# Chaining the partial sums of the seven Strassen-Winograd products in PSUM, with a ScalarE copy from bank to bank

## Chip, cores and metric

The kernel runs on one core of a Trainium2 chip. The metric is the device time of one execution in microseconds (us), median of three runs.

## The reference

Two transformer layers over 1024 tokens of 1024 features, in float32: forgetting attention, SwiGLU, retention, SwiGLU, each behind an RMS norm and with a residual, and a last norm. The change touches the SwiGLU stages and the projections of the retention:

```python
def swiglu(h, w_in, w_out):
    gu = h @ w_in
    return (jax.nn.silu(gu[..., :D_FF]) * gu[..., D_FF:]) @ w_out      # D_FF = 2816

def retention(h, w_in, w_out):
    proj = h @ w_in                          # q 1024, k 1024, v 2048, g 2048 columns
    q, k, v, g = ...                         # 4 heads; q and k are rotated
    ...                                      # chunkwise recurrence
    return (jax.nn.silu(g) * y) @ w_out
```

## The kernel before

Every operand is the sum of two float32r tiles, `hi` and `lo`. `split` writes them: ScalarE casts `hi` (L98), VectorE subtracts to get `lo` (L99). A product of two operands is three matmuls (hi·hi, hi·lo, lo·hi), lines L638, L639 and L640. Weights come by DMA into `st` tiles (five buffers) and are split into `wh` and `wl` tiles (six buffers each), 512 columns at a time. Activations are split into `b` tiles, which stay for a whole stage.

The large matrix products go by Strassen-Winograd. The weights of a pair of 128-column tiles are four blocks A11, A12, A21, A22 with the sums S1 to S4; the activations are four blocks B11 to B22 with the sums T1 to T4. Seven products of twelve matmuls (128x128 weights on 512 tokens) make the four blocks of the result C11, C12, C21, C22. Three PSUM banks take them: A11·B11 and A12·B21 accumulate in bank a, which is C11; S2·T2, S3·T3 and A22·T4 accumulate in bank b; S1·T1 and S4·B22 in bank c. The order is the table `PRODUCTS`: A11, S2, S1, S3, A12, S4, A22.

Bank b holds no result by itself. P1, the first product, belongs to C12, C21 and C22 too. So ScalarE copies bank a after its first product into an SBUF tile `p1` (L699), and VectorE adds `p1` to what bank b holds after S2 (`u2`, L702), after S3 (`u3`, L706) and after A22 (L713). Bank c is added after S1 (L708) and after S4 (L711).

`pair_T` does so for the 22 pairs of each SwiGLU's first matrix (`ffn`, 44 in all) and for 16 pairs of the retention's projections (`rotated`, `gates`). `pair_N` does the same token-major with 256-column weights for the values (4 pairs, two banks for each of a, b, c; L737 to L739). `pair_acc` and `paired_out` do the second SwiGLU matrix, whose activations are kept in memory as sums (`Stored`) and come back through `st` tiles: two groups of four pairs for each SwiGLU, `first` telling the group that writes the sums `y` (copies by ScalarE, L653) from the one that adds to them (VectorE, L650).

Banks come from one pool of seven in turn (`mm_ps`); three are in use for a pair. The program is written in dependence order; a scheduler of the language sets the order of the instructions on each engine, and each engine runs its own list in order.

Of the kernel before, what the change touches and what calls it, by code (L numbers as in the profile page):

```python
# [17 lines left out]
P = 128  # L18
# [19 lines left out]
def trunk(ctx, tc, nc, d, out):  # L38
# [145 lines left out]
    # =================== forgetting attention ===================  # L184
    with ExitStack() as fs:
# [230 lines left out]
        # the keys of the first two heads, a pass over the features as they come  # L416
# [79 lines left out]
    # where the sums of a phase are kept  # L496
# [41 lines left out]
    class Stored:  # L538
        """The sums of a group of four pairs of feature tiles, kept in memory, split at their first use."""
# [29 lines left out]
    class Blocks:  # L569
        """The four blocks of a pair of column tiles and their sums, split on demand."""  # L570
# [25 lines left out]
        def get(self, n):  # L596
# [13 lines left out]
            if n == "S4":  # L610
# [4 lines left out]
    PRODUCTS = (("A11", "B11", "a"), ("S2", "T2", "b"), ("S1", "T1", "c"), ("S3", "T3", "b"),  # L615
                ("A12", "B21", "a"), ("S4", "B22", "c"), ("A22", "T4", "b"))

    class Products:
        """The seven products of one pair of 128-column tiles, feature-major."""

        def __init__(self, src, X):
            self.w, self.X, self.banks = src if isinstance(src, Blocks) else Blocks(src), X, {}

        def __call__(self, i):
            n, t, bk = PRODUCTS[i]
            if n == "S2" and not self.w.s1:
                self.w.sums()
            hi, lo = self.w.get(n)
            tt = self.X.get(t)
            new = bk not in self.banks  # L630
            if new:
                self.banks[bk] = mm_ps()
            ps = self.banks[bk]
            for j in range(4):
                js = slice(j * P, (j + 1) * P)
                th, tl = tt[j]
                f = new and j == 0
                nc.tensor.matmul(ps, hi[:, js], th, start=f, stop=False, skip_group_check=not new)  # L638
                nc.tensor.matmul(ps, hi[:, js], tl, start=False, stop=False, skip_group_check=not new)  # L639
                nc.tensor.matmul(ps, lo[:, js], th, start=False, stop=(j == 3), skip_group_check=not new)  # L640

    def pair_acc(src, X, y, first):
        """Adds the products of one pair to the sums y over the groups of feature tiles."""
        prod = Products(src, X)
        banks = prod.banks
        if first:
            y.update({n: yu(n) for n in ("11", "12", "21", "22")}, p=qu("p"))

        def add(n, bk):
            nc.vector.tensor_tensor(y[n], banks[bk], y[n], op=ALU.add)  # L650

        def put(n, bk):
            nc.scalar.copy(y[n], banks[bk]) if first else add(n, bk)  # L653

        prod(0)
        put("p", "a")
        prod(1)
        put("12", "b")
        prod(2)
        prod(3)  # L660
        put("22", "b")
        add("22", "c")
        prod(4)
        put("11", "a")
        prod(5)
        add("12", "c")
        prod(6)
        put("21", "b")

    def paired_out(wsrc, stored, scale_rows, xold):  # L670
        """x + (scaled) act @ W over the groups of eight feature tiles whose sums are in memory."""
        ys = [{} for _ in range(4)]
        out = [[None, None] for _ in range(KT)]
        for g, X in enumerate(stored):
            for n in range(4):
                y = ys[n]
                pair_acc(wsrc[g, n], X, y, g == 0)
                if g < len(stored) - 1:
                    continue
                for q in ("12", "21", "22"):  # L680
                    nc.vector.tensor_tensor(y[q], y[q], y["p"], op=ALU.add)
                for i in range(2):
                    for h in range(2):
                        u = y[f"{i + 1}{h + 1}"]
                        if scale_rows:
                            nc.vector.tensor_tensor(u, u, R[:, HALF[h]], op=ALU.mult)
                        xo = sp.tile([P, H], F32, tag="xo", name=nm("xo"), bufs=2)
                        nc.sync.dma_start(xo, xold[2 * n + i][:, HALF[h]])
                        nc.vector.tensor_tensor(u, u, xo, op=ALU.add)
                        out[2 * n + i][h] = u  # L690
        return out

    def pair_T(src, X):
        """Feature-major C11, C12, C21, C22 of one pair of 128-column tiles."""
        prod = Products(src, X)
        banks = prod.banks
        prod(0)
        p1 = yu("p1")
        nc.scalar.copy(p1, banks["a"])  # L699
        prod(1)  # L700
        u2 = yu("u2")
        nc.vector.tensor_tensor(u2, banks["b"], p1, op=ALU.add)  # L702
        prod(2)
        prod(3)
# [4 lines left out]
        prod(4)  # L709
        prod(5)  # L710
        nc.vector.tensor_tensor(u2, banks["c"], u2, op=ALU.add)  # L711
        prod(6)
        nc.vector.tensor_tensor(p1, banks["b"], p1, op=ALU.add)  # L713
        return banks["a"], u2, p1, c22, u3

    def pair_N(srcs, X):
        """Token-major C11, C12, C21, C22 of one pair of 256-column tiles, as two tiles of two token blocks."""
        ws = [Blocks(s) for s in srcs]
        banks = {}

        def prod(n, t, bk):
            parts = [w.get(n) for w in ws]
            new = bk not in banks
            if new:
                banks[bk] = [mm_ps(), mm_ps()]
            for s in range(2):
                ps = banks[bk][s]
                for b in range(2):
                    o = ps[:, b * 256:(b + 1) * 256]
                    tk = slice((2 * s + b) * P, (2 * s + b + 1) * P)  # L730
                    for j in range(4):
                        hi, lo = parts[j // 2]
                        js = slice(j % 2 * 256, (j % 2 + 1) * 256)
                        th, tl = X.get(t)[j]
                        f = new and j == 0 and b == 0
                        sk = not (new and b == 0)
                        nc.tensor.matmul(o, th[:, tk], hi[:, js], start=f, stop=False, skip_group_check=sk)  # L737
                        nc.tensor.matmul(o, th[:, tk], lo[:, js], start=False, stop=False, skip_group_check=sk)  # L738
                        nc.tensor.matmul(o, tl[:, tk], hi[:, js], start=False, stop=(j == 3), skip_group_check=sk)  # L739

        prod(*PRODUCTS[0])
        p1 = [yu("p1"), yu("p1")]
        for s in range(2):
            nc.scalar.copy(p1[s], banks["a"][s])
        for w in ws:
            w.sums()
        prod(*PRODUCTS[1])
        u2, u3, c22 = [[yu(x), yu(x)] for x in ("u2", "u3", "c22")]
        for s in range(2):
            nc.vector.tensor_tensor(u2[s], banks["b"][s], p1[s], op=ALU.add)  # L750
        prod(*PRODUCTS[2])
        prod(*PRODUCTS[3])
        for s in range(2):
            nc.vector.tensor_tensor(u3[s], banks["b"][s], p1[s], op=ALU.add)
            nc.vector.tensor_tensor(c22[s], banks["c"][s], u3[s], op=ALU.add)
        prod(*PRODUCTS[4])
        prod(*PRODUCTS[5])
        for s in range(2):
            nc.vector.tensor_tensor(u2[s], banks["c"][s], u2[s], op=ALU.add)
        prod(*PRODUCTS[6])  # L760
        for s in range(2):
            nc.vector.tensor_tensor(p1[s], banks["b"][s], p1[s], op=ALU.add)
            nc.scalar.copy(u3[s], banks["a"][s])
        return u3, u2, p1, c22
# [489 lines left out]
```

## Time and profile before

| | |
|---|---|
| runs | 2626.6, 2627.21, 2629.64 us (median 2627.21) |
| profiled execution, span of the trace | 2626.0 us |
| median of the runs less that span | 1.2 us |
| TensorE busy | 2600.0 us (99%) |
| VectorE busy | 1960.2 us (75%) |
| ScalarE busy | 1155.9 us (44%) |
| 490 to 910, 1960 to 2375 us | first matrix of the two SwiGLUs |
| 910 to 1075, 2375 to 2545 us | second matrix, paired part |
| 1150 to 1610 us | projections of the retention |

The span is the time from the first to the last instruction of one profiled execution; the profile gives no other time of it. Busy time of an engine is the union of its instructions; a matmul's end is modelled, so TensorE counts as busy as long as matmuls follow each other closely.

### The profile page before, as it was taken

To read this page: it belongs to the slowest core of one execution; us is meant where nothing else is said; L and a number is where in the kernel's file an instruction comes from. 1 tells how busy PE (TensorE), PEld (TensorE's weight loads), DVE (VectorE), ACT (ScalarE), POOL (GpSimd) and SP (SyncE) were. 2 spreads that over 40 slices of the span, in tenths; PEclk is the share of its full clock that TensorE was granted. 3 is DMA by queue.
4 is the path that set the end of the run, shared out by engine and by line. 5 is a ranking of instruction groups with operands and counts; after the bars stand their busy time and mean duration, and the time that the engine had idled before them with its cause. 6 is when DMAs were issued, how large, how long until landed. Compare 5 with 4: busy or idle time off the path is not lost.

```text
span 2626.0 us, 35148 instructions
## 1 busy us (share of the span) xinstructions
PE 2600.0 (99%) x12808; PEld 2179.9 (83%) x12808; DVE 1960.2 (75%) x3367; ACT 1155.9 (44%) x2168; POOL 167.6 (6%) x147
## 2 busy tenths in 40 slices
PE   9999999999999999999999999999999999999998
PEld 8878887888888878889898989898888888887888
DVE  6798888877767778987667676885567776768795
ACT  6566666533233444453333425662353233335533
POOL 0143322000000000001000010000000000000000
PEclk9999999999999999999999999999999999999999
DMA  3111143332332345533332325655522332325441
GB/s 129 44 57 65 49 145 119 122 106 95 109 104 97 109 152 180 167 107 117 104 113 96 113 101 160 189 196 192 190 85 85 104 111 86 109 84 183 156 158 65
DMA packets 137694, 312.11 MB, mean 119 GB/s; under 512 B 15665, under 2 KB 28721, under 8 KB 137521
## 3 DMA queue, kind: packets, MB, share of 16 engines
q1 hardware_dynamic: 136800, 309.33, 35.1%
q8 instruction: 100, 1.64, 0.3%
q14 instruction: 74, 0.60, 0.1%
q10 hardware_dynamic: 720, 0.55, 0.1%
HBM read 217.54 MB, written 92.27 MB: 118 GB/s over the span
## 4 chain that ended last, share of the span: by engine, by line
PE 89%; DMA 4%; DVE 3%; issue 2%; ACT 1%; POOL 0%; SPq 0%; DVEq 0%; POOLq 0%; ACTq 0%
PE mm L638 17%; PE mm L640 17%; PE mm L639 17%; PE mm L106 7%; PE mm L107 7%; PE mm L108 7%; PE mm L738 2%; PE mm L739 2%; PE mm L737 2%; DMA st<-vd 1%; DMA st<-ac_T 1%; PE mm L256 1%; PE mm L258 1%; PE mm L257 1%; DVE b L99 1%
## 5 line engine op out<-in xcount | busy, mean ns | idle before, releaser
L639 PE MATMUL mm<-b,wh 128*128 128x512 f32 x2128 | 836.8, 394 | 0.0
L638 PE MATMUL mm<-b,wh 128*128 128x512 f32 x2128 | 832.9, 395 | 3.2 <-ACT 22_4397_22190 L653 1.8
L640 PE MATMUL mm<-b,wl 128*128 128x512 f32 x2128 | 819.5, 394 | 0.1
L98 ACT CAST wh<-st 128x512 fp32r<-128x512 f32 (+1 forms) x449 | 275.2, 616 | 578.4 <-PE mm L639 409.4
L638 PEld LDWEIGHTS mm<-b,wh 128*128 128x128 f32 x2128 | 400.3, 188 | 97.8 <-ACT 22_4397_22190 L653 2.2
L640 PEld LDWEIGHTS mm<-b,wl 128*128 128x128 f32 x2128 | 399.8, 188 | 94.1 <-DVE wl L99 0.9
L639 PEld LDWEIGHTS mm<-b,wh 128*128 128x128 f32 x2128 | 400.0, 188 | 91.9 <-DVE b L99 0.2
L99 DVE TENSOR_TENSOR wl<-st,wh 128x512 fp32r<-128x512 f32 (+1 forms) x449 | 311.5, 697 | 55.8 <-ACT wh L98 51.8
L98 ACT CAST wh<-s 128x512 fp32r<-128x512 f32 x252 | 156.0, 621 | 413.3 <-PE mm L639 356.8
L106 PE MATMUL mm<-b,wh 128*128 128x512 f32 x736 | 289.7, 397 | 8.4 <-ACT b L126 5.7
L107 PE MATMUL mm<-b,wh 128*128 128x512 f32 x736 | 290.0, 395 | 1.4 <-DVE b L99 1.4
L108 PE MATMUL mm<-b,wl 128*128 128x512 f32 x736 | 289.9, 395 | 0.0
L99 DVE TENSOR_TENSOR wl<-s,wh 128x512 fp32r<-128x512 f32 x252 | 182.6, 727 | 41.4 <-ACT wh L98 39.7
L106 PEld LDWEIGHTS mm<-b,wh 128*128 128x128 f32 x736 | 138.9, 189 | 40.5 <-ACT b L126 6.5
L107 PEld LDWEIGHTS mm<-b,wh 128*128 128x128 f32 x736 | 138.8, 189 | 32.0 <-DVE b L99 1.8
L108 PEld LDWEIGHTS mm<-b,wl 128*128 128x128 f32 x736 | 138.7, 188 | 31.5
L98 ACT CAST b<-st 128x512 fp32r<-128x512 f32 (+1 forms) x216 | 125.1, 612 | 81.7 <-DMA st<-ac_T 30.0
L99 DVE TENSOR_TENSOR b<-st,b 128x512 fp32r<-128x512 f32 (+1 forms) x216 | 140.0, 674 | 27.9 <-ACT b L98 22.5
L711 DVE TENSOR_TENSOR u<-mm,u 128x512 f32<-128x512 f32 x60 | 41.4, 689 | 116.1 <-PE mm L640 115.9
L738 PE MATMUL mm<-wl,b 128*128 128x256 f32 x448 | 126.0, 281 | 0.0
L739 PE MATMUL mm<-wh,b 128*128 128x256 f32 x448 | 125.9, 281 | 0.0
L737 PE MATMUL mm<-wh,b 128*128 128x256 f32 x448 | 125.8, 281 | 0.0
(514 smaller groups left out, 3965.2 us busy)
## 6 DMA issues: line engine op xcount, KB each, us to landing
st<-ffn_in SPq DMA_DIRECT2D x88, 512.0 KB, 3.5
st<-ffn_out_pairs SPq DMA_DIRECT2D x32, 512.0 KB, 5.4
st<-ac_T SPq DMA_DIRECT2D x32, 512.0 KB, 4.6
ac_T<-t SPq DMA_DIRECT2D x48, 256.0 KB, 2.4
st<-ac_B SPq DMA_DIRECT2D x24, 512.0 KB, 4.6
st<-fox_qk SPq DMA_DIRECT2D x32, 256.0 KB, 2.7
xo<-xd SPq DMA_DIRECT2D x32, 256.0 KB, 3.1
ac_B<-p SPq DMA_DIRECT2D x32, 256.0 KB, 3.1
```

Of the source, the lines that this page charges most:

```text
L98: nc.scalar.copy(hi, src)
L99: return nc.vector.tensor_tensor(lo, src, hi.bitcast(F32), op=ALU.subtract)
L106: nc.tensor.matmul(ps, wh, xh, start=(first and k == 0), stop=False)
L107: nc.tensor.matmul(ps, wh, xl, start=False, stop=False)
L108: nc.tensor.matmul(ps, wl, xh, start=False, stop=(last and k == n - 1))
L638: nc.tensor.matmul(ps, hi[:, js], th, start=f, stop=False, skip_group_check=not new)
L639: nc.tensor.matmul(ps, hi[:, js], tl, start=False, stop=False, skip_group_check=not new)
L640: nc.tensor.matmul(ps, lo[:, js], th, start=False, stop=(j == 3), skip_group_check=not new)
L711: nc.vector.tensor_tensor(u2, banks["c"], u2, op=ALU.add)
L737: nc.tensor.matmul(o, th[:, tk], hi[:, js], start=f, stop=False, skip_group_check=sk)
L738: nc.tensor.matmul(o, th[:, tk], lo[:, js], start=False, stop=False, skip_group_check=sk)
L739: nc.tensor.matmul(o, tl[:, tk], hi[:, js], start=False, stop=(j == 3), skip_group_check=sk)
```

## The change

The seven products keep their operands. Their order and the place of the sums change. After A11 ScalarE copies bank a into bank b, from PSUM to PSUM (L642 of the kernel after), and S2, S3 and A22 accumulate onto that copy, so that bank b holds P1+S2, then P1+S2+S3, then all four. `u2` and `u3` are then ScalarE copies of bank b in between (L669, L666), and VectorE adds only bank c to them. C11 and C21 are read from the banks by whoever uses them, and no `p1` tile is left. The order of a pair becomes A11, copy, S1, S2, copy `u2`, A12, S3, copy `u3`, then A11 of the next pair (`open`), and only then A22 and S4 (`close`). `pair_N`'s order is A11, S1, S2, A12, S3, A22, S4. In the retention the values of a head come after all of its four feature-major pairs; they came between the third and the fourth.

```diff
-    PRODUCTS = (("A11", "B11", "a"), ("S2", "T2", "b"), ("S1", "T1", "c"), ("S3", "T3", "b"),
-                ("A12", "B21", "a"), ("S4", "B22", "c"), ("A22", "T4", "b"))
+        def open(self):
+            self.a, self.c, self.b = mm_ps(), mm_ps(), mm_ps()
+            self.run("A11", self.a, first=True)
+            nc.scalar.copy(self.b, self.a)
+            return self
+
+        def middle(self, u2, u3):
+            self.run("S1", self.c, first=True)
+            self.run("S2", self.b)
+            u2(self.b)
+            self.run("A12", self.a)
+            self.run("S3", self.b)
+            u3(self.b, self.c)
+
+        def close(self):
+            self.run("A22", self.b)
+            self.run("S4", self.c)
+
+    def in_turn(srcs, X, use):
+        n = len(srcs)
+        cur = Products(srcs[0], X).open()
+        for i in range(n):
+            u2, u3 = yu("u2"), yu("u3")
+            def closed(b, c):
+                nc.scalar.copy(u3, b)
+                nc.vector.tensor_tensor(u3, c, u3, op=ALU.add)
+            cur.middle(lambda b: nc.scalar.copy(u2, b), closed)
+            nxt = Products(srcs[i + 1], X).open() if i < n - 1 else None
+            cur.close()
+            nc.vector.tensor_tensor(u2, cur.c, u2, op=ALU.add)
+            use(i, cur.a, u2, cur.b, u3)
+            cur = nxt
...
-        prod(0)
-        p1 = yu("p1")
-        nc.scalar.copy(p1, banks["a"])
-        prod(1)
-        u2 = yu("u2")
-        nc.vector.tensor_tensor(u2, banks["b"], p1, op=ALU.add)
-        prod(2)
-        prod(3)
-        u3 = yu("u3")
-        nc.vector.tensor_tensor(u3, banks["b"], p1, op=ALU.add)
-        c22 = yu("c22")
-        nc.vector.tensor_tensor(c22, banks["c"], u3, op=ALU.add)
-        prod(4)
-        prod(5)
-        nc.vector.tensor_tensor(u2, banks["c"], u2, op=ALU.add)
-        prod(6)
-        nc.vector.tensor_tensor(p1, banks["b"], p1, op=ALU.add)
-        return banks["a"], u2, p1, c22, u3
...
+        prod.middle(lambda b: put("12", b), closed)
+        put("11", prod.a)
+        nx = nxt() if nxt else None
+        prod.close()
+        put("21", prod.b)
+        nc.vector.tensor_tensor(y["12"], prod.c, y["12"], op=ALU.add)
+        return nx
...
     for h in range(RET_HEADS):
-        rotated(nw if h == 0 else d["ret_qk"][1 + 2 * h], kd[h])
-        gates(2 * h)
-        rotated(d["ret_qk"][2 * h], qd[h])
+        srcs = [nw if h == 0 else d["ret_qk"][1 + 2 * h], d["ret_g"][2 * h], d["ret_qk"][2 * h], d["ret_g"][2 * h + 1]]
+        in_turn(srcs, X, lambda i, *cc: projected(4 * h + i, *cc))
         values(h)
-        gates(2 * h + 1)
```

In the built programs the matmuls are the same number (12660), VectorE's tensor-tensor instructions go from 3079 to 2843, ScalarE's copies and casts from 1350 to 1486; the DMAs are the same number.

ScalarE's list in the middle of the first SwiGLU matrix before: casts of weights (`wh`), one copy of bank a to `p` for a pair, one activation (`u`).

```order
L98 CAST wh_6574<-st_6570 128x512
L98 CAST wh_6597<-s_1350_6594 128x512
L98 CAST wh_6616<-s_1349_6593 128x512
L98 CAST wh_6634<-st_6572 128x512
L98 CAST wh_6654<-st_6570 128x512
L699 COPY p_1348_6591<-mm_6578 128x512
L820 ACTIVATE u_1335_6509<-u_1335_6509 128x512
```

The same place after. `mm_6368` and `mm_6229` are the banks b of a pair and of the pair before it, `mm_6366` is the bank a of the first; `wh_6480` takes the buffer of the weights of the S3 product of the pair before.

```order
L98 CAST wh_6447<-s_1321_6443 128x512
L669 COPY u_1292_6288<-mm_6229 128x512
L98 CAST wh_6463<-s_1322_6444 128x512
L98 CAST wh_6480<-st_6362 128x512
L642 COPY mm_6368<-mm_6366 128x512
L98 CAST wh_6497<-st_6364 128x512
L666 COPY u_1293_6289<-mm_6229 128x512
L816 ACTIVATE t_6420<-t_6420 128x512
```

Three copies of banks stand there for each pair where one stood, and one of them, into the next pair's bank b, stands behind a weight cast that waits for a buffer.

The second place is ScalarE's list where the second SwiGLU's second matrix begins, before: `b` casts of sums that come back from memory (`st`), then the copy of bank b to `22`.

```order
L98 CAST b_22392<-st_22390 128x512
L98 CAST b_22396<-st_22390 128x512
L98 CAST b_22402<-st_22400 128x512
L98 CAST b_22406<-st_22400 128x512
L98 CAST b_22429<-st_22427 128x512
L98 CAST b_22433<-st_22427 128x512
L98 CAST b_22439<-st_22437 128x512
L98 CAST b_22443<-st_22437 128x512
L653 COPY 22_4397_22190<-mm_22258 128x512
```

The same change of stage after:

```order
L98 CAST b_22215<-st_22213 128x512
L666 COPY u_4328_21929<-mm_21865 128x512
L98 CAST b_22219<-st_22213 128x512
L816 ACTIVATE t_22036<-t_22036 128x512
L98 CAST wh_22209<-st_22049 128x512
L98 CAST b_22225<-st_22223 128x512
L642 COPY mm_22053<-mm_22051 128x512
L98 CAST b_22229<-st_22223 128x512
```

The copy into bank b of the first paired products (`mm_22053`) now stands behind casts of sums loaded from memory, as the copy to `22` did; the last sums (T4, B22) are cast later than before, against the products that need them.

## Rows read from the trace of the kernel before

**Rows 1.** The page: span, busy time by engine, granted TensorE clock in 40 slices.

```profile
span 2626.0 us, 35148 instructions
...
PE 2600.0 (99%) x12808; PEld 2179.9 (83%) x12808; DVE 1960.2 (75%) x3367; ACT 1155.9 (44%) x2168; POOL 167.6 (6%) x147
...
PEclk9999999999999999999999999999999999999999
```

**Rows 2.** Windows by stage: length, busy us (count) by engine, granted clock, DMA share, GB/s.

```profile
490.00:910.00 420.00, 419.98 (x1830) 341.07 (x1829) 305.64 (x503) 142.57 (x242) 0.00 (x0) 1.00 0.28 97
910.00:1075.00 165.00, 163.97 (x705) 132.07 (x704) 137.88 (x226) 80.26 (x144) 0.00 (x0) 1.00 0.51 166
...
1150.00:1610.00 460.00, 459.88 (x2659) 402.90 (x2657) 327.61 (x508) 169.73 (x366) 50.30 (x32) 1.00 0.33 108
...
1960.00:2375.00 415.00, 414.60 (x1808) 337.03 (x1807) 300.82 (x496) 137.95 (x235) 0.00 (x0) 1.00 0.29 97
2375.00:2545.00 170.00, 168.21 (x725) 135.75 (x724) 141.64 (x234) 81.73 (x147) 0.00 (x0) 1.00 0.51 167
```

**Rows 3.** Waits of TensorE: total us, times, longest us.

```profile
PE mm L106 <- ACT b L126: 5.7, 2, 5.5
...
PE mm L638 <- ACT 22_4397_22190 L653: 1.8, 1, 1.8
...
PE mm L638 <- ACT 22_1738_8786 L653: 0.9, 1, 0.9
...
PE mm L638 <- ACT wh L98: 0.4, 1, 0.4
...
PE mm L638 <- DVE 12_1832_9061 L650: 0.2, 1, 0.2
```

**Rows 4.** Timeline of TensorE at the longest of these (start, length).

```profile
2400.56 0.39 PE L639 MATMUL mm<-b,wh 128*128 128x512 f32 x1
2400.79 0.39 PE L640 MATMUL mm<-b,wl 128*128 128x512 f32 x1
2402.97 0.50 PE L638 MATMUL mm<-b,wh 128*128 128x512 f32 x1 [1.79 <-ACT 22_4397_22190 L653]
```

**Rows 5.** Timeline of ScalarE at the same place.

```profile
2397.30 1.15 ACT L98 CAST b<-st 128x512 fp32r<-128x512 f32 x2 [0.68 <-DMA st<-ac_T]
2401.30 1.14 ACT L98 CAST b<-st 128x512 fp32r<-128x512 f32 x2 [2.85 <-DMA st<-ac_T]
2402.34 0.58 ACT L653 COPY 22_4397_22190<-mm 128x512 f32<-128x512 f32 x1
```

**Rows 6.** Waits of ScalarE for the sums that come back from memory.

```profile
ACT b L98 <- DMA st<-ac_T: 30.0, 21, 2.9
```

**Rows 7.** Groups of VectorE from 500 to 910 us: count, busy us, mean ns, idle before.

```profile
L702 DVE TENSOR_TENSOR u<-mm,p 128x512 f32<-128x512 f32 x22 | 15.1, 686 | 16.5 <-PE mm L640 16.5
...
L706 DVE TENSOR_TENSOR u<-mm,p 128x512 f32<-128x512 f32 x21 | 14.5, 690 | 21.5 <-PE mm L640 21.5
...
L713 DVE TENSOR_TENSOR p<-mm,p 128x512 f32<-128x512 f32 x21 | 14.4, 683 | 0.3 <-PE mm L640 0.3
```

**Rows 8.** Groups of ScalarE from 500 to 910 us.

```profile
L98 ACT CAST wh<-st 128x512 fp32r<-128x512 f32 x84 | 52.2, 622 | 142.9 <-PE mm L639 130.1 <-issue 12.8
...
L699 ACT COPY p<-mm 128x512 f32<-128x512 f32 x21 | 12.1, 579 | 0.0
```

**Rows 9.** Windows with little and with much VectorE work.

```profile
950.00:1000.00 50.00, 50.00 (x217) 40.53 (x216) 29.35 (x47) 24.07 (x45) 0.00 (x0) 1.00 0.36 118
1050.00:1100.00 50.00, 50.00 (x217) 40.52 (x216) 44.23 (x76) 20.50 (x36) 0.00 (x0) 1.00 0.55 169
```

**Rows 10.** Timeline of ScalarE in the first SwiGLU matrix.

```profile
704.74 0.63 ACT L98 CAST wh<-st 128x512 fp32r<-128x512 f32 x1 [1.66 <-PE mm L639]
705.27 0.58 ACT L699 COPY p<-mm 128x512 f32<-128x512 f32 x1
705.75 0.63 ACT L820 ACTIVATE u<-u 128x512 f32<-128x512 f32 x1
```

More of the change, by code (lines that the diff above doesn't have):

```diff
@@ L613, in get, with run @@
             return wsplit(self.a22)
-    PRODUCTS = (("A11", "B11", "a"), ("S2", "T2", "b"), ("S1", "T1", "c"), ("S3", "T3", "b"),
-                ("A12", "B21", "a"), ("S4", "B22", "c"), ("A22", "T4", "b"))
+    OPERANDS = {"A11": "B11", "S1": "T1", "S2": "T2", "A12": "B21", "S3": "T3", "A22": "T4", "S4": "B22"}
     class Products:
         def __init__(self, src, X):
[L622 to L626, printed above, removed]
+            self.w, self.X = src if isinstance(src, Blocks) else Blocks(src), X
+        def run(self, n, ps, first=False, last=False):
+            if n in ("S1", "S2") and not self.w.s1:
                 self.w.sums()
             hi, lo = self.w.get(n)
[L629 to L633, printed above, removed]
+            tt = self.X.get(OPERANDS[n])
             for j in range(4):
@@ L636, in __call__ @@
                 th, tl = tt[j]
[L637 to L645, printed above, removed]
+                nc.tensor.matmul(ps, hi[:, js], th, start=first and j == 0, stop=False, skip_group_check=True)
@@ L646, in pair_acc @@
+    def pair_acc(prod, nxt, y, first):
         if first:
-            y.update({n: yu(n) for n in ("11", "12", "21", "22")}, p=qu("p"))
-        def add(n, bk):
-            nc.vector.tensor_tensor(y[n], banks[bk], y[n], op=ALU.add)
+            y.update({n: yu(n) for n in ("11", "12", "21", "22")})
         def put(n, bk):
-            nc.scalar.copy(y[n], banks[bk]) if first else add(n, bk)
-        prod(0)
-        put("p", "a")
-        prod(1)
-        put("12", "b")
-        prod(2)
-        prod(3)
@@ L661, in pair_acc, with closed @@
-        put("22", "b")
-        add("22", "c")
-        prod(4)
-        put("11", "a")
-        prod(5)
-        add("12", "c")
-        prod(6)
-        put("21", "b")
+            nc.scalar.copy(y[n], bk) if first else nc.vector.tensor_tensor(y[n], bk, y[n], op=ALU.add)
+        def closed(b, c):
+            put("22", b)
+            nc.vector.tensor_tensor(y["22"], c, y["22"], op=ALU.add)
+        prod.middle(lambda b: put("12", b), closed)
+        put("11", prod.a)
+        nx = nxt() if nxt else None
@@ L673, in paired_out @@
         out = [[None, None] for _ in range(KT)]
[L674 to L690, printed above, removed]
@@ L691, in paired_out @@
[L691 to L714 removed]
+        todo = [(g, n) for g in range(len(stored)) for n in range(4)]
@@ new lines, in paired_out @@
+        prod = Products(wsrc[0, 0], stored[0]).open()
+        for i, (g, n) in enumerate(todo):
+            y = ys[n]
+            nxt = todo[i + 1] if i + 1 < len(todo) else None
+            prod = pair_acc(prod, (lambda: Products(wsrc[nxt[0], nxt[1]], stored[nxt[0]]).open()) if nxt else None, y, g == 0)
+            if g < len(stored) - 1:
+                continue
+            for i in range(2):
+                for h in range(2):
+                    u = y[f"{i + 1}{h + 1}"]
+                    if scale_rows:
+                        nc.vector.tensor_tensor(u, u, R[:, HALF[h]], op=ALU.mult)
+                    xo = sp.tile([P, H], F32, tag="xo", name=nm("xo"), bufs=2)
+                    nc.sync.dma_start(xo, xold[2 * n + i][:, HALF[h]])
+                    nc.vector.tensor_tensor(u, u, xo, op=ALU.add)
+                    out[2 * n + i][h] = u
@@ L716, in pair_N, with prod @@
+        return out
     def pair_N(srcs, X):
         ws = [Blocks(s) for s in srcs]
-        banks = {}
-        def prod(n, t, bk):
+        a, c, b = [[mm_ps(), mm_ps()] for _ in range(3)]
+        u2, u3 = [[yu(x), yu(x)] for x in ("u2", "u3")]
+        def prod(n, bank, first=False, then=None):
+            if n in ("S1", "S2"):
+                for w in ws:
+                    if not w.s1:
+                        w.sums()
             parts = [w.get(n) for w in ws]
-            new = bk not in banks
-            if new:
-                banks[bk] = [mm_ps(), mm_ps()]
+            tt = X.get(OPERANDS[n])
@@ L726, in prod @@
             for s in range(2):
[L727 to L730, printed above, removed]
+                for q in range(2):
+                    o = bank[s][:, q * 256:(q + 1) * 256]
+                    tk = slice((2 * s + q) * P, (2 * s + q + 1) * P)
                     for j in range(4):
@@ L733, in prod @@
                         js = slice(j % 2 * 256, (j % 2 + 1) * 256)
[L734 to L764, printed above, removed]
+                        th, tl = tt[j]
+                        f = first and j == 0 and q == 0
+                        nc.tensor.matmul(o, th[:, tk], hi[:, js], start=f, stop=False, skip_group_check=True)
@@ new lines, in prod, with closed @@
+                        nc.tensor.matmul(o, th[:, tk], lo[:, js], start=False, stop=False, skip_group_check=True)
+                        nc.tensor.matmul(o, tl[:, tk], hi[:, js], start=False, stop=(j == 3), skip_group_check=True)
+                if then:
+                    then(s)
+        def closed(s):
+            nc.scalar.copy(u3[s], b[s])
+            nc.vector.tensor_tensor(u3[s], c[s], u3[s], op=ALU.add)
+        prod("A11", a, True, lambda s: nc.scalar.copy(b[s], a[s]))
+        prod("S1", c, True)
@@ L766, in wtile2 @@
+        prod("S2", b, False, lambda s: nc.scalar.copy(u2[s], b[s]))
+        prod("A12", a)
+        prod("S3", b, False, closed)
+        prod("A22", b)
+        prod("S4", c, False, lambda s: nc.vector.tensor_tensor(u2[s], c[s], u2[s], op=ALU.add))
+        return a, u2, b, u3
     def wtile2(src, nk):
@@ L814, in ffn, with gated @@
         stored = [Stored(f"ac{i}_{g}_", pools) for g in range(2)]
-        for f in range(FT):
-            c11, c12, c21, c22, t = pair_T(nw if f == 0 and nw else d["ffn_in"][i, f], X)
+        even = []
+        def gated(f, c11, c12, c21, c22):
             if f == 0:
                 rms(nrm, mp, "ms")
+            t = yu("t")
             nc.vector.tensor_tensor(t, c11, R[:, HALF[0]], op=ALU.mult)
@@ L951, in values, with gates @@
         nc.vector.tensor_scalar(m, m, -1.0 / 512, None, op0=ALU.mult)
-    def gates(p):
-        c11, c12, c21, c22, t = pair_T(d["ret_g"][p], X)
+    def gates(p, c11, c12, c21, c22):
         if p == 0:
```

40 lines of the change are left out of this document (25 added, 15 removed).

## The prediction

> **What bounds the kernel now.** I read the page first. TensorE is busy for 2600.0 of 2626.0 us, its granted clock is at the top level of 2.4 GHz in all 40 slices, and VectorE (75%) and ScalarE (44%) are far from full [rows 1]. Then the windows, cut at the stages that the change touches: TensorE is busy for 419.98 of 420.00 us in the first SwiGLU matrix, 163.97 of 165.00 in its second, 459.88 of 460.00 in the retention's projections, 414.60 of 415.00 and 168.21 of 170.00 in the second SwiGLU [rows 2]. The idle time of the five stages is 0.02 + 1.03 + 0.12 + 0.40 + 1.79 = 3.4 us. That is the first number to take away: a change of sums that leaves the matmuls as they are has 3.4 us of waiting to win in all its stages. The list of TensorE's waits says the same by another way: its long ones belong to other stages (5.7 us at L106), and the four groups at L638, a line of the seven products, hold 1.8 + 0.9 + 0.4 + 0.2 = 3.3 us [rows 3].
>
> A matmul of 512 columns starts 0.23 us after the one before it [rows 4], so a product of twelve takes 2.77 us and a pair of seven 19.4 us. I use 0.23 us and not the 0.39 us that the trace gives as one matmul's length, since they overlap.
>
> **The change, part by part.** *VectorE's adds of P1.* The built programs have 236 fewer: 3 for each of the 44 and 16 pairs of `pair_T`, 6 for each of 4 `pair_N`, 32 in the paired stages, 180 + 24 + 32. One takes 683 to 690 ns [rows 7], so VectorE loses 236 x 0.69 = 163 us of its 1960. What lies over all of it is the matmul stream: in the first SwiGLU window VectorE works 305.64 us while TensorE has 0.02 us idle [rows 2]. Gain on the path: 0. VectorE's own waits show it from the other side: the adds L702 and L706 wait for TensorE (16.5 and 21.5 us), not it for them [rows 7].
>
> *ScalarE's copies.* There are 136 more, at 0.58 us [rows 8] about 79 us; ScalarE goes from 44% to some 47%. A copy from PSUM to PSUM is in no row of before. Nearest is the copy PSUM to SBUF, 579 ns, and the cast between SBUF tiles, 622 ns [rows 8]. I take 0.58 us, since like it the copy reads PSUM, with half of it and the VectorE add's 0.69 us [rows 7] as ends; neither fills ScalarE. The page "ScalarE: Activation LUTs" of the Trainium skill, section "Step-by-step: what each stage is for", says that ScalarE writes PSUM with less latency than SBUF; by it the copy would be a little shorter than 0.58 us, which the lower end holds already.
>
> *The wait that the copy adds in steady state.* The copy to bank b stands between A11 and S2 of a pair, and TensorE can't begin S2 without it. Queued ahead of it on ScalarE is one weight cast, which waits until the S3 of the pair before has released a weight buffer. In the tightest half of the pattern that S3 comes right behind A11, then twelve matmuls of S1, then S2. So after S3 there is 2.77 us, and ScalarE needs the cast and the copy: their starts stand 0.53 us apart and the copy lasts 0.58 us [rows 10], together 1.1 us; with the cast itself waiting for the end of S3's last matmul but one, about 1.3 us. Slack: 1.5 us, and in the other half of the pattern, where 24 matmuls lie between, over 4 us. `u2` and `u3` have the same picture: the copy must be done before S3 or A22 writes on, with another product (2.77 us) in between. If the copy took 0.7 us the slack would still be 1.4. I take 0 for the steady state. If the cover went, that is, if S2 were next on TensorE behind A11, each copy would cost 0.58 us.
>
> *The stalls of before.* The longest, 1.8 us, is at 2400.79: the next matmul starts 2.18 us after the last, because bank b's copy to `22` comes late [rows 4], and it is late because on ScalarE it stands behind two casts that waited 2.85 us for sums from memory [rows 5]. The stall of 0.9 us is its twin in the first SwiGLU. Afterwards these casts (of T4 and B22) come later against the copy, since T4's product now follows the A11 of the next pair: products of 2.77 us lie between. The four groups of 3.3 us go.
>
> *What is late next.* In the new order of ScalarE the copy into bank b of the first paired products stands behind casts of sums loaded from memory, the very thing that made `22` late, and so do the copy to `12` and the second pair's copy at some places. ScalarE waits for such loads 21 times for 30.0 us, 1.43 us a wait, 2.9 at most [rows 6]. I price the two changes of stage (near 915 and 2380 us) at one mean wait each on the path, 2 x 1.43 = 2.9 us. The ends are 0 (TensorE has other products issued ahead) and two copies late by 2.9 us at each, 4 x 2.9 = 11.6 us. In the retention, the last feature-major pair now hands over to `pair_N` with its copies behind a weight cast; by the same count of 1.3 us against 2.77 there is no wait, and if there were one, four heads at the cast and copy would give 4 x 1.3 = 5.2 us.
>
> *The sum*, against the profiled span of 2626.0: 2626.0 - 3.3 + 2.9 = 2625.6 us. The median of the runs stands 1.2 us above that span, so 2626.8, as good as the median of before, 2627.2. I say 2627.
>
> **The rivals.** *No measurable change* (the sum above): chance 0.70. A measurement of this kernel can tell about 0.2%, or 5.3 us, from no change.
>
> *Slower: copies queued behind loads.* ScalarE's list is in order, and three copies of banks now hang on it where one did, each of which a later product waits for. Place: the two changes of stage and the four hand-overs of the retention. Price: 11.6 + 5.2 - 3.3 gives 2626.0 + 13.5 + 1.2 = 2640.7 us if all of it shows; it decides (over 5.3 us) once the new waits exceed 8.6 us, that is, six mean waits of 1.43. For it: the stall at 2400.79 is this mechanism [rows 5]. Against: it happened in two places of two stages in before, for 2.7 us together. Chance 0.17, at about 2634.
>
> *Slower: every pair waits for the copy.* The seven products of a pair use one chain in bank b: A11, copy, S2, copy, S3, copy, A22. If TensorE met the copy each time, the 84 copies into b (44 + 16 + 16 pairs and 4 x 2 of the values) at 0.58 us would give 49 us, 2675 us. Against it speaks the slack of 1.5 us, and that the order puts a product of another bank between each copy and its reader. Chance 0.05. The Trainium skill, "Perfetto Trace Analysis", section "Matmuls", has a rule that speaks against such a chain: independent groups of matmuls should go through different PSUM banks, so that emptying one bank overlaps the next group. By that rule the time would be this rival's; the trace of before bears it out only so far that TensorE stalls where a bank's copy is late [rows 4], and the new order does keep banks a and c, and the next pair's, between.
>
> *Faster: matmuls follow each other more closely when VectorE reads PSUM less.* The 44 + 16 + 16 pairs hold 76 x 7 x 12 = 6384 matmuls of 512 columns; 0.82 ns less for each would be 5.3 us and decide. For it there would have to be a difference now, between stretches with little and with much VectorE work. There is none that counts show: 217 matmuls in 50 us at 29.35 us of VectorE's work and 217 at 44.23 [rows 9]. Less than one matmul in 217 is under 0.23 us / 217 = 1.06 ns for 15 us of work in 50; the change takes 3 x 0.69 = 2.1 us in 19.4, or 5.4 in 50. So at most 0.4 ns a matmul, 2.5 us, 2624 us. Together with stalls that vanish and none in their place (2626.0 - 3.3 - 2.5 + 1.2 = 2621.4) it only just reaches 0.2%. Chance of over 0.2%: 0.08.
>
> **How the numbers follow.** 0.08 faster, 0.70 same, 0.17 + 0.05 = 0.22 slower. The likeliest case's own range is 2624 (no new wait) to 2631. The range for 8 in 10 begins at the lower bound of the faster case, 2621, and reaches to the middle of the queued copies, 2636; above it lie the 2675 us and the upper part of the queued copies, about 0.1 together.
>
> **What would show it.** Right: TensorE still at 99% with the same granted clock; the waits at the first matmul line of the seven products 2 to 6 us in all, for copies into bank b, near 915 and 2380 us; VectorE's busy time down to about 1800 us and ScalarE's up to about 1235; in 490 to 910 us no idle time worth a row; still 217 matmuls in 50 us. Wrong: many waits of TensorE for the bank copy in the middle of a SwiGLU matrix (the chain in one bank), waits over 3 us each at the stage changes or at the retention's hand-overs (the queued copies), or 218 or more matmuls in 50 us (closer matmuls).

## The result: 0.3% slower

Median 2635.99 us (9 runs, 2631.55 to 2637.27) against 2627.2 us before (9 runs): ratio 1.0032, 95% interval 1.0022 to 1.0041. I had forecast no change at 2627 us; the time lies at the upper edge of my range, and the case that came, a slower kernel, is the one I gave a chance of 0.22. Two executions, one each in experiments 6 and 7, ran at a mean granted clock of 0.654 and 0.801 and took 3660.07 and 2996.44 us; the medians and ratios below leave them out.

The profiled execution spans 2634.9 us, 8.9 more than before. The page after, span, busy time by engine and granted clock, to be read against [rows 1]:

```profile
span 2634.9 us, 35097 instructions
...
PE 2601.4 (99%) x12808; PEld 2184.5 (83%) x12808; DVE 1838.5 (70%) x3131; ACT 1221.3 (46%) x2304; POOL 165.9 (6%) x147
...
PEclk9999999999999999999999999999999999999999
```

VectorE lost 236 instructions and 122 us of busy time, ScalarE gained 136 and 65 us, TensorE worked as long as before. The page does not show where the 8.9 us are; the windows by stage do (the columns are those of [rows 2]):

```profile
490.00:910.00 420.00, 420.00 (x1830) 341.38 (x1829) 275.40 (x441) 165.91 (x286) 0.00 (x0) 1.00 0.29 98
910.00:1075.00 165.00, 160.11 (x682) 129.45 (x681) 126.90 (x205) 81.01 (x147) 0.00 (x0) 0.98 0.49 161
...
1150.00:1610.00 460.00, 460.00 (x2598) 401.12 (x2598) 290.06 (x446) 186.59 (x386) 49.18 (x32) 1.00 0.32 106
1610.00:1960.00 350.00, 344.41 (x1805) 296.61 (x1804) 232.02 (x467) 171.80 (x365) 0.00 (x0) 1.00 0.52 175
1960.00:2375.00 415.00, 415.00 (x1812) 338.00 (x1811) 271.39 (x432) 159.26 (x277) 0.00 (x0) 1.00 0.29 95
2375.00:2545.00 170.00, 168.93 (x730) 137.01 (x730) 135.08 (x218) 87.75 (x159) 0.00 (x0) 1.00 0.52 170
```

Where the seven products run in their steady pattern, TensorE is never idle. The loss stands in two places: 4.9 us of idle time between 910 and 1075 us, at a granted clock of 0.98, and 5.6 us in the retention's core (0.9 us before). TensorE's waits after name them (total us, times, longest):

```profile
PE mm L635 <- DVE 22_1731_8782 L682: 4.9, 1, 4.9
PE mm L1083 <- ACT wh L1072: 2.9, 1, 2.9
...
PE mm L1032 <- ACT b L1017: 1.6, 1, 1.6
...
PE mm L635 <- ACT 22_4499_22622 L682: 1.1, 1, 1.1
PE mm L1012 <- DVE wl L1073: 1.0, 1, 1.0
```

The four waits of the seven products in [rows 3] (3.3 us) are gone. One of 4.9 us and one of 1.1 us have come at the same line's successor, L635, and the other three belong to the retention's core.

Both traces hold 12808 matmuls, so the time at which the n-th begins can be compared. Where the order within the retention's projections differs, such a number means nothing, so the table skips them.

| n-th matmul | before us | after us | after less before | step |
|---|---|---|---|---|
| 400 | 75.3 | 76.4 | +1.1 | start of the program, the same code in both |
| 4400 | 917.8 | 918.4 | +0.5 | -0.6: all else up to the end of the first SwiGLU's first matrix |
| 4800 | 1011.9 | 1011.1 | -0.8 | -1.3: the stall near 935 us is gone |
| 5200 | 1105.2 | 1111.1 | +5.9 | +6.7: the stall at 1016 us |
| 5400 | 1151.7 | 1157.2 | +5.5 | -0.4 |
| 9400 | 1864.5 | 1875.2 | +10.7 | +5.1: the retention's projections and the first part of its core |
| 11600 | 2370.4 | 2380.1 | +9.7 | -1.0: up to the end of the second SwiGLU's first matrix |
| 11800 | 2418.8 | 2426.4 | +7.6 | -2.1: the stall at 2400 us is gone |
| 12000 | 2465.2 | 2474.0 | +8.8 | +1.2: a stall at 2471 us |
| last | 2619.8 | 2628.0 | +8.3 | -0.5; another 0.6 behind the last matmul |

**The stall at 1016 us.** TensorE's timeline:

```profile
1016.21 0.40 PE L636 MATMUL mm<-b,wh 128*128 128x512 f32 x1
1016.45 0.40 PE L637 MATMUL mm<-b,wl 128*128 128x512 f32 x1
1021.73 0.76 PE L635 MATMUL mm<-b,wh 128*128 128x512 f32 x1 [4.89 <-DVE 22_1731_8782 L682]
1022.29 0.63 PE L636 MATMUL mm<-b,wh 128*128 128x512 f32 x1
1022.72 0.63 PE L637 MATMUL mm<-b,wl 128*128 128x512 f32 x1
```

The matmul that waits is the first of A22 in the first pair of the second group. It writes bank b, from which VectorE must first have added P1+S2+S3 to `22`; in the second group this hand-over is a VectorE add and not a ScalarE copy (`put`, L682). What VectorE did meanwhile:

```profile
1012.38 0.69 DVE L99 TENSOR_TENSOR b<-st,b 128x512 fp32r<-128x512 f32 x1
1014.73 0.69 DVE L99 TENSOR_TENSOR b<-st,b 128x512 fp32r<-128x512 f32 x1 [1.66 <-ACT b L98]
...
1017.29 0.69 DVE L99 TENSOR_TENSOR b<-st,b 128x512 fp32r<-128x512 f32 x1
1017.90 0.68 DVE L682 TENSOR_TENSOR 11_1728_8779<-mm,11_1728_8779 128x512 f32<-128x512 f32 x1
...
1019.70 0.68 DVE L712 TENSOR_TENSOR 11_1728_8779<-11_1728_8779,R 128x512 f32<-128x512 f32 x1
1020.30 0.69 DVE L588 TENSOR_TENSOR s<-st 128x512 f32<-128x512 f32 x1
1020.90 0.68 DVE L682 TENSOR_TENSOR 22_1731_8782<-mm,22_1731_8782 128x512 f32<-128x512 f32 x1
```

Bank b was ready at 1014.0 us, twelve matmuls before the stall. VectorE was idle then, waiting in order for ScalarE's cast of a loaded sum (`b`), and from 1014.73 us it worked through splits of loaded sums and of weights, `12`, `11` and its scaling, one every 0.6 us. The add stood behind ten of these. It is the end of a queue that got moving late, not a slow instruction. ScalarE's cast, in this execution and in a second one of the same kernel (experiment 9, stall 5.4 us):

```profile
1014.08 1.14 ACT L98 CAST b<-st 128x512 fp32r<-128x512 f32 x2 [2.25 <-PE mm L637]
```

```profile
1014.23 1.14 ACT L98 CAST b<-st 128x512 fp32r<-128x512 f32 x2 [3.25 <-DMA st<-ac_B]
```

In the second it waited for the load. In the first the load landed at 1014.00 us and the matmul that is named ended at 1014.04, so either would have held it.

The add was late in the kernel before, too, and nothing showed it there:

```profile
1016.38 0.68 DVE L650 TENSOR_TENSOR 22_1738_8786<-mm,22_1738_8786 128x512 f32<-128x512 f32 x1
```

These views leave out which bank it is; the order in which the program was built tells it. In the kernel before, S3's last matmul ended at 1012.0 us, the add began 4.4 us later, and it ended 0.5 us ahead of A22's first matmul, since 24 matmuls lay between S3 and A22. After, the add begins 6.9 us behind S3's end and 12 matmuls lie between. So A22 came 2.8 us nearer and the add 2.5 us later; less the 0.5 us that were to spare, that makes 4.8 us of the 4.9.

The clock made the stall dearer: behind it one gap is 0.56 us, nine are 0.43 us and one is 0.30 us, not 0.23, which adds 2.1 us.

**The retention's core.** ScalarE before the wait of 1.6 us at 1631.30:

```profile
1627.73 0.42 ACT L945 ACTIVATE u<-u 128x256 f32<-128x256 f32 x1 [1.42 <-DVE u L757]
...
1630.16 0.72 ACT L993 ACTIVATE b<-st,vmean 128x512 fp32r<-128x512 f32 x1 [1.53 <-DMA st<-vd]
1630.79 0.46 ACT L1017 ACTIVATE b<-mm,kap 128x256 fp32r<-128x256 f32 x1
```

L945 is the last head's values, still on their way to memory while the core (L993, L1017) has begun to load values from there. Before, a pair of gates came last, and the values lay one pair further back. The longest wait, 2.9 us, ends with a cast of ScalarE (L1072) that stands behind casts of loaded keys:

```profile
1641.14 0.62 ACT L98 CAST b<-st 128x512 fp32r<-128x512 f32 x1 [0.83 <-DMA st<-kd]
...
1641.86 0.57 ACT L1072 ACTIVATE wh<-mm,kap 128x384 fp32r<-128x384 f32 x1
```

### The profile page after: what moved, and what is told of

Same layout as the page of the kernel before. It is cut to its first block, busy times and chain, and to the rows that moved or that the text cites. A ratio compares the mean times of both kernels' runs of the same rounds, so it can differ in the third digit from the quotient of the medians.

```text
span 2634.9 us, 35097 instructions
## 1 busy us (share of the span) xinstructions
PE 2601.4 (99%) x12808; PEld 2184.5 (83%) x12808; DVE 1838.5 (70%) x3131; ACT 1221.3 (46%) x2304; POOL 165.9 (6%) x147
## 4 chain that ended last, share of the span: by engine, by line
PE 92%; DMA 2%; DVE 2%; ACT 1%; issue 1%; POOL 0%; SPq 0%; DVEq 0%; POOLq 0%; ACTq 0%
PE mm L636 18%; PE mm L635 18%; PE mm L637 18%; PE mm L106 7%; PE mm L107 7%; PE mm L108 7%; PE mm L743 2%; PE mm L742 2%; PE mm L741 2%; DMA st<-vd 1%; PE mm L256 1%; PE mm L258 1%; PE mm L257 1%; PE mm L1084 1%; PE mm L1085 1%
## 5 line engine op out<-in xcount | busy, mean ns | idle before, releaser
L635 PE MATMUL mm<-b,wh 128*128 128x512 f32 x2128 | 836.7, 394 | 6.0 <-DVE 22_1731_8782 L682 4.9
L637 PE MATMUL mm<-b,wl 128*128 128x512 f32 x2128 | 837.2, 395 | 0.0
L635 PEld LDWEIGHTS mm<-b,wh 128*128 128x128 f32 x2128 | 401.5, 189 | 98.2 <-issue 5.3
L108 PE MATMUL mm<-b,wl 128*128 128x512 f32 x736 | 290.6, 396 | 0.0
L99 DVE TENSOR_TENSOR b<-st,b 128x512 fp32r<-128x512 f32 x216 | 140.8, 678 | 35.1 <-ACT b L98 32.6
L98 ACT CAST b<-st 128x512 fp32r<-128x512 f32 x216 | 124.9, 611 | 86.0 <-DMA st<-ac_T 30.9
L588 DVE TENSOR_TENSOR s<-st 128x512 f32<-128x512 f32 x84 | 58.0, 691 | 67.9 <-DMA st<-ffn_in 25.1
```

What stands on the lines that cost most here:

```text
L98: nc.scalar.copy(hi, src)
L99: return nc.vector.tensor_tensor(lo, src, hi.bitcast(F32), op=ALU.subtract)
L108: nc.tensor.matmul(ps, wl, xh, start=False, stop=(last and k == n - 1))
L588: nc.vector.tensor_tensor(self.s1, self.a21, self.a22, op=ALU.add)
L635: nc.tensor.matmul(ps, hi[:, js], th, start=first and j == 0, stop=False, skip_group_check=True)
```

## Experiments

Each ratio is against the kernel before on the same chip, whose median was 2625.1 to 2626.4 us in these sessions.

**1. The paired part undone.** `pair_acc` and `paired_out` as before, everything else as after.

```diff
-        prod.middle(lambda b: put("12", b), closed)
...
+        prod(0)
+        put("p", "a")
+        prod(1)
+        put("12", "b")
...
```

> The kernel after, with the paired part of both SwiGLUs (second matrix) as before: P1 in SBUF, order A11, S2, S1, S3, A12, S4, A22; the first matrix and the retention stay chained. If the loss near 1016 us comes from that part (A22 waits for the add of bank b to 22, one product behind S3): the 4.9 us wait and the slow matmuls behind it (6.7 us together) and the 1.1 us near 2471 go, the waits of before near 935 and 2400 us (1.0 and 2.0) come back: 2634.9 - 6.7 - 1.2 + 3.0 = 2630.0 us of span, 2631 us median. If the loss comes from ScalarE's load by the chained copies in general: no stage gets faster, 2636.

Median 2629.49 us, ratio 1.0013 (1.0004 to 1.0022). Near 1016 us two short waits are left, 0.63 us for a cast of weights and 0.08 us for the add to `22`. So the stall came with the paired part, and ScalarE's load in general did not make it. By the built order the add is late here as well, 6.1 us, with nothing chained in the paired part; 24 matmuls cover it. One point missed: the waits near 935 and 2400 us did not come back. The scheduler built 22 and 14 matmuls between S3 and A22 there and not 12 as in the kernel before, so the new sums of the paired part are not needed to take them away.

**2. The values third again.**

```diff
-        in_turn(srcs, X, lambda i, *cc: projected(4 * h + i, *cc))
+        in_turn(srcs[:3], X, lambda i, *cc: projected(4 * h + i, *cc))
         values(h)
+        in_turn(srcs[3:], X, lambda i, *cc: projected(4 * h + 3, *cc))
```

> The kernel after, with the values of a head between the third and the fourth feature-major pair, as before, so that a pair of gates and not the values come last ahead of the retention's core. If the waits of the core's first 80 us (1629, 1639, 1692 us: 5.4 us more than before) come from the values' copies and stores falling into it: they go back to about 1.4 us, span 2634.9 - 5.4 = 2629.5, median 2630.5; the first 1600 us do not change. If they come from the chained copies: unchanged, 2636.

Median 2631.43 us, ratio 1.0014 (1.0005 to 1.0023); span 2629.7, as expected to 0.2 us. The first 120 us around the core, here:

```profile
1600.00:1720.00 120.00, 118.17 (x672) 104.75 (x672) 92.56 (x206) 80.04 (x175) 0.00 (x0) 1.00 0.55 173
```

in the kernel before:

```profile
1600.00:1720.00 120.00, 119.07 (x671) 104.98 (x671) 94.59 (x220) 77.26 (x172) 0.00 (x0) 1.00 0.55 175
```

and in the kernel after, 3.8 us less of TensorE than here, at a lower clock:

```profile
1600.00:1720.00 120.00, 114.41 (x720) 104.08 (x720) 80.30 (x185) 75.32 (x180) 0.00 (x0) 0.99 0.52 167
```

The stall at 1016 us stays (4.9 us). The chained copies are not what the core waits for.

**3. Only the order of the values, in the kernel before.**

```diff
-        values(h)
         gates(2 * h + 1)
+        values(h)
```

> The kernel before with one thing of the change alone: the values of a head after its four feature-major pairs. If the order of the values makes the core's waits: about 5 us longer than before, 2632 us median, with waits of TensorE at 1610 to 1700 us as after. If the chained sums make them: 2627 us, as before.

Median 2637.08 us, ratio 1.0036 (1.0024 to 1.0049): as slow as the whole change, with nothing chained. The same window and the core's longest wait:

```profile
1600.00:1720.00 120.00, 111.50 (x689) 100.58 (x688) 83.22 (x192) 74.86 (x178) 0.00 (x0) 0.99 0.52 167
```

```profile
PE mm L1029 <- ACT b L1014: 6.1, 2, 3.6
```

Direction as expected, size not: 11 us and not 5. In the profiled execution 8.8 us of it stand between the 5400th and the 9400th matmul, where the kernel after has 5.1. L1029 is in this kernel what L1032 is in the one after, so it waits for the same operation of ScalarE.

**4. The second group as before.** Chained sums in the first group, P1 to SBUF and the old order in the second, where the old order has A12 and S4 between S3 and A22.

```diff
...
+            pair_add(wsrc[g, n], stored[g], y, False)
+            for q in ("12", "21", "22"):
+                nc.vector.tensor_tensor(y[q], y[q], y["p"], op=ALU.add)
```

> The kernel after, with only the second group of the paired part (both SwiGLUs) as before: P1 to SBUF, order A11, S2, S1, S3, A12, S4, A22, so that two products and not one lie between S3 and A22; the first group stays chained. If nearness of S3 and A22 made the stall at 1016 us: it goes with the slow matmuls behind it, 6.7 us, and the waits near 935 and 2400 us stay away: span 2628.2, median 2629.3. If VectorE's queue alone makes it whatever the distance: a wait of about 5 us stays near 1016 us, 2636.

Median 2627.66 us, ratio 1.0005 (0.9996 to 1.0013); span 2626.9. The stage that lost 4.9 us:

```profile
910.00:1075.00 165.00, 165.00 (x712) 133.48 (x711) 135.91 (x222) 81.97 (x148) 0.00 (x0) 1.00 0.50 165
```

The stall is gone, without any other change there than the second group's sums and order. By the built order the add to `22` begins 4.8 us behind S3's end here, with 24 matmuls between S3 and A22.

**5. Four copies in place of one**, in the first matrix of both SwiGLUs.

```diff
-            nc.scalar.copy(self.b, self.a)
+            for _ in range(copies):
+                nc.scalar.copy(self.b, self.a)
```

> The kernel after, with the copy of bank a into bank b made four times in a row in the first matrix of both SwiGLUs (the result is the same). It tells how much slack S2 has behind the copy. By the prediction 1.5 us in the tight half of the pattern: three more copies start 0.5 us apart, so 1.5 us more, and TensorE just begins to wait: under 0.2 us in each second pair, 0 to 4 us over the 44 pairs, and no wait in the others. If the slack were 0, as the rule of one chain in one bank has it, each pair would lose 1.5 us, 66 us over the 44.

One run, 2638.82 us. The first matrix:

```profile
490.00:910.00 420.00, 420.00 (x1828) 341.49 (x1827) 273.02 (x442) 199.62 (x353) 0.00 (x0) 1.00 0.29 99
```

ScalarE works 34 us longer there and TensorE does not wait, so the copy costs nothing in the steady pattern. By the built order the copies start 0.61 us apart, and in the tight half of the pattern the fourth ends 2.6 us ahead of S2's first matmul; in the kernel after the one copy ends 4.4 us ahead of it. This kernel shows something else too: at 2492 us it has the twin of the stall at 1016 us, in the second SwiGLU.

```profile
PE mm L635 <- DVE 22_4364_22226 L683: 3.3, 1, 3.3
```

The kernel after has no such wait there. By the built order it has 27 matmuls between S3 and A22 at that place and an add that is 5.1 us late; here there are 24 and the add is 8.1 us late. Distance and lateness decide together, and both change with the order that the scheduler builds.

**6. Both mended**: the edits of 2 and 4 together.

> The kernel after with both edits that gave time back: the values of a head between its third and fourth pair, and the second group of the paired parts with P1 in SBUF. If the two losses are independent: the span of the second-group edit, 2626.9, less the core's waits that it still had (5.5 us, about 1.5 stay): 2622.5 to 2623, median 2624, 0.1% under before. If the order of the values only moves waits about: 2627, as before.

Median 2622.3 us (ten runs), ratio 0.9986 (0.9977 to 0.9996): under both kernels, by 0.14% and 0.5%. The two gains add up, so the losses are independent. The second groups are not chained here. What is left in the two places:

```profile
910.00:1075.00 165.00, 165.00 (x712) 133.44 (x711) 135.88 (x223) 81.47 (x147) 0.00 (x0) 1.00 0.50 165
...
1600.00:1720.00 120.00, 119.44 (x680) 105.97 (x679) 94.89 (x223) 80.30 (x176) 0.00 (x0) 1.00 0.53 172
```

**7. Chained, with S3 further from A22.** In the second group only, S3 ahead of A12.

```diff
-            self.run("A12", self.a)
+            if not far:
+                self.run("A12", self.a)
             self.run("S3", self.b)
             u3(self.b, self.c)
+            if far:
+                self.run("A12", self.a)
...
-        prod.middle(lambda b: put("12", b), closed)
+        prod.middle(lambda b: put("12", b), closed, not first)
```

> The kernel after, all sums chained, with one edit: in the second group of the paired parts S3 comes before A12, so that in the built order 20 matmuls (4.6 us) and not 12 (2.8 us) lie between the end of S3 and A22, and the add of bank b to 22 stands four places earlier on VectorE (about 2.4 us). If the stall near 1016 us is nearness and VectorE's queue, not the chain: the wait of 4.9 us shrinks by 1.8 to 4.3 us and the slow matmuls behind it (2 us) go: 4 to 6.5 us faster than after, median 2630 to 2632. If the chain itself makes it: 4.9 us and 2636 stay.

The profiled span is 2630.8 us and the wait at 1016 us has shrunk to 2.5 us, with no slow matmuls behind it (granted clock 1.00 from 1016 to 1026 us, 0.67 in the kernel after):

```profile
1016.00:1026.00 10.00, 7.49 (x33) 5.78 (x33) 10.00 (x18) 4.42 (x8) 0.00 (x0) 1.00 0.37 117
```

```profile
1016.00:1026.00 10.00, 5.11 (x14) 3.78 (x13) 9.73 (x17) 3.18 (x6) 0.00 (x0) 0.67 0.61 196
```

By the built order the add is still 6.3 us late; eight more matmuls between, 1.9 us, shorten the wait most. The edit brings waits of its own, 0.5 us at 1009 us and, in the second SwiGLU, where 13 matmuls lie between, this one at 2492 us:

```profile
PE mm L635 <- DVE 22_4364_22094 L685: 1.4, 1, 1.4
```

But the median is 2635.4 us (five runs), ratio 1.0035 (1.0023 to 1.0047), level with after. Profile and median disagree.

**8. The same with the values third.**

> The edit of the run before and the values of a head between its third and fourth pair: the whole change with chained sums everywhere, only the order mended. If both losses are matters of order: 2636 - 5.4 - (4 to 6.5) = 2624 to 2626.5 median, level with or just under before, and about 2 us above the version that undoes the second group.

Median 2627.78 us, ratio 1.0007 (0.9998 to 1.0016). Experiment 2, which lacks only the edit of 7, had 2631.43 us and 1.0014 in another session: 2 to 4 us more, as the profile of 7 would have it, though the intervals overlap.

**9 and 10. The kernel after and the kernel of 7 again, on one chip.**

> The kernel after once more, on the same chip as the next one, since the median of the chained second group with S3 earlier (2635.6 us of five runs) did not follow its profile (wait of 2.5 us in place of 4.9). Expected 2636 us median, the wait near 1016 us again 4 to 5 us with slow matmuls behind it; if the wait differs by more than 2 us between two profiles of one kernel, single profiles tell too little of it.

> The chained second group with S3 before A12 again, beside the kernel after. If nearness and VectorE's queue make the stall: 3 to 4 us faster than after on this chip (2632), wait near 1016 us 1 to 3 us. If the edit only looked good in one profile: level with after.

The median of the five runs of 7 is 2635.4 us, not the 2635.6 named above. After: 2634.91 us, ratio 1.0033 (1.0021 to 1.0045), the wait at 1016 us again 5.4 us. The edit: 2635.65 us, ratio 1.0032 (1.002 to 1.0045), wait 2.4 us, profiled span 2630.0. So the shorter stall repeats in the profile, and the median again does not follow. Of both sessions together the edit has ten runs in two groups, four of 2631.8 to 2632.6 us, the profiled ones among them, and six of 2635.4 to 2638.1; those with the lowest mean granted clock, 0.996 and 0.997, are among the longer. What the longer executions do I can't say, since none was profiled. The runs of the kernel after spread as far, 2631.55 to 2637.27 us, and its two profiled ones, 2636.74 and 2635.7 us, are not among its shortest. So the spans, 4 us apart, compare a short execution of one kernel with a longer one of the other, and that the edit saves time is not shown; that the wait is shorter is, in both profiles.

## Why the prediction was wrong

**What was right.** The adds of P1 gave no time back, because the matmuls lie over them. The bank-to-bank copy takes 580 ns (I took 0.58 us):

```profile
L642 ACT COPY mm<-mm 128x512 f32<-128x512 f32 x21 | 12.2, 580 | 0.2 <-PE mm L637 0.2
```

TensorE does not meet it in the steady pattern: idle time 0.00 us in 420 and in 415 us, and with four copies still none. The slack that I counted for it, 1.5 us, was too small. I had the copy stand behind a cast that waits for S3; by the built order it begins 0.4 us behind A11's end, before S3 has ended, and is done 4.4 us ahead of S2 in the tight half. The 2675 us that I drew from the rule of the Trainium skill ("Perfetto Trace Analysis", section "Matmuls"), that independent groups of matmuls should go through different banks, did not come: other banks' products stand between each copy and its reader, which is the overlap that the rule asks for. The old stalls of 3.3 us did go. By the built order 12 matmuls lay between S3 and A22 near 935 and 2400 us before, with the copy to `22` 3.0 and 3.9 us late; after, 24 lie between and it is 1.5 and 0.4 us late. Matmuls do not follow each other more closely: 1830 in the 420 us of the first matrix in both kernels, and 217 in 50 us at 31 us of VectorE's work, as with 44 in [rows 9].

```profile
550.00:600.00 50.00, 50.00 (x217) 40.57 (x216) 31.34 (x49) 17.54 (x31) 0.00 (x0) 1.00 0.31 106
```

Busy time moved less than I worked out (VectorE 122 us and not 163, ScalarE 65 and not 79): it is a union, and instructions back to back start 0.6 and 0.48 us apart. That accounts for ScalarE (136 x 0.48 = 65); for VectorE it gives 142, and the other 20 us stay unexplained. It changed nothing in the time.

**The steps that failed.** *"What is late next"* priced late hand-overs at 2.9 us, for ScalarE copies at the changes of stage near 915 and 2380 us. There was none there. They came one step further on, at the change of group and in the middle of the second SwiGLU's paired part, and the dear one was on VectorE: 6.7 us at 1016 us and 1.2 us at 2471 us. (At 2471 us it is ScalarE's copy to `22`, 2.3 us behind S3's end, with 8 matmuls between by the built order.) I had looked at the queues that the new copies join (ScalarE), and took an add that the change leaves where it was for harmless. But the change had moved its reader. Before, two products stand in program order between S3, whose sum the add reads from bank b, and A22, which writes on in that bank; after, there is one, the next pair's A11, 2.77 us. In the built orders the 24 matmuls became 12. My sentence that `u2` and `u3` *"have the same picture"* holds for the copies of the steady pattern; for the add in the second group it does not. Nor did I look how late that add was before: 4.4 us, with 0.5 us to spare. Experiments 1 and 4 show that the stall belongs to the second group's sums and order, and the profiles of 7, 8 and 10 that with more matmuls between S3 and A22 the wait is halved with the chain kept.

*The hand-over to `pair_N`* was the only thing I priced of the values' new place, at 0 to 5.2 us, and it did cost nothing: TensorE is never idle from 1150 to 1610 us. What I left out is what comes behind the last values: the retention's core, 5.1 us. I listed the move as part of the change and then never asked which work it puts next to which. Experiment 2 took it away, 3 made it alone.

So my rival "slower: copies queued behind loads" had the kind of mechanism right, engines' lists in order behind loads, and both of its places wrong. The likelier case was wrong by the two terms above: 2626.8 - 2.9 + 6.7 + 1.2 + 5.1 = 2636.9 us against 2636.74 us of the profiled execution. That it fits to 0.2 us is luck: the other steps of the table come to about -0.8 us, and this execution took 1.8 us more than its span, where my sum has 1.2.

**What stays open.** Why the add came 2.5 us later behind S3 than before: VectorE's list, the loads and S3's own time all moved. Why, with the stall halved, most executions of 7 are not faster than after. And why the values' order alone cost 11 us in the kernel before but 5 in the one after.

## What to carry to other kernels

When TensorE is at 99%, as here, a change that frees 120 us of another engine wins little and can shift the waits, so look for the hand-over that it brings nearer to its reader, above all the ones whose code it does not touch. For each bank or buffer count the work between the read that must end and the write that waits, before and after, in the order that was built; read from the trace of before how late that read already is; and then see what stands ahead of the read in its engine's list where data comes late. A reordering that comes along with the main idea is an edit of its own: cost what it now puts next to each other, and try it alone; here, made alone, it was as dear as the whole change. With the values' order undone and the second groups unchained the kernel was 0.14% faster than before; with everything chained and both orders mended (experiment 8) it was level with it.

## What the runs showed of the hardware

I had not expected the clock to add to a wait. Behind the stall of 4.89 us ten matmuls of 512 columns start 0.43 us apart, and the granted clock of 1016 to 1026 us is 0.67, a mix of the levels 1.2 and 2.4 GHz; behind the wait of 1.79 us in [rows 4] that trace has them 0.23 us apart again from the second on. Matmuls at 0.43 us follow the core's wait of 2.9 us, too (1644.11 to 1645.82 us). The stall, 5.1 us from start to start, so cost 7.2. A ScalarE copy from PSUM to PSUM takes 580 ns, as one to SBUF (581 and 582 ns in the same window):

```profile
L669 ACT COPY u<-mm 128x512 f32<-128x512 f32 x21 | 12.2, 582 | 0.0
L666 ACT COPY u<-mm 128x512 f32<-128x512 f32 x21 | 12.2, 581 | 0.0
```

The page "ScalarE: Activation LUTs" of the Trainium skill, section "Step-by-step: what each stage is for", calls PSUM the faster destination; in these rows there is no difference to speak of.
